# Two early steps of the down projection beside the last channel tile, and that tile's convolution moved behind the third step's operands

## The chip, the core and the metric

The kernel runs on one core of a Trainium2 chip. It uses TensorE (PE, matrix products into PSUM), VectorE (DVE), ScalarE (ACT), GpSimd (POOL) and the sync engine's queue (SP), which issues most of the DMAs. Each engine takes its own instructions strictly in the order in which they stand in its queue and waits at an instruction until what it needs is there. The metric is device microseconds of one execution, the median of several runs, lower is better.

## What is computed

One encoder layer over 256 prompt tokens and 1024 sample tokens of width 1024: a mixer, then a convolutional gated feed-forward network, each with its norms and gated residual. The change lies in the second half:

```python
def conv_ffn(h, w_up, w_conv, b_conv, w_down):
    up = h @ w_up                                   # 1024 -> 2 * 2816 channels
    up = depthwise_conv_of_width_3(up, w_conv) + b_conv
    gate, val = jnp.split(up, 2, axis=-1)
    return (jax.nn.silu(gate) * val) @ w_down       # 2816 -> 1024
```

## The kernel before

**Products in two halves.** Every float32 operand is split in two fp32r parts, a rounded "hi" part (written by ACT, line 90) and the remainder "lo" (written by POOL or DVE, line 91). A product is three matmuls: hi by hi, hi by lo, lo by hi. An operand is complete when both parts are written, and the second or third matmul waits for the lo part.

**The up stage** (lines 1161 to 1257) walks over 22 channel tiles of 128 channels, f. For the sample tokens, which are held in two halves of 512, the two by two block product of weights and tokens is done with seven products of 12 matmuls each instead of eight (a Strassen form with weight sums S1 to S4, tiles `S`). The order on PE is X, Y, X, V, X, V, X: the PSUM banks X and V are accumulated further after they have been copied out, so the next product into a bank waits for the copy. ACT copies X to `ug` (lines 1221 and 1227), V to `uv` (1229) and X again (1237), DVE adds Y to `ug` (1223), X to `uv` (1231), V to `ug` (1233). Then comes the convolution: ACT makes `ag` and `av` with the middle tap (line 1050), DVE adds two taps to each (line 1046, four instructions of 128x1023), ACT applies Silu to `ag` (1247), DVE multiplies (1249), and the product goes to DRAM as `g_d[f]` (line 1079). Tiles 10 to 21 come first, with the prompt tokens merged in, then tiles 0 to 9; tile 9 is the last.

**The down stage** (lines 1259 on) is again a Strassen form, over token halves by column halves: seven products M3, M5, M1, M7, M4, M2, M6, each of which sums over 11 steps k (channel tiles 2k and 2k+1) with 5 token tiles of three matmuls, 15 matmuls for a step. For each step `ops_of` loads the `A` tile of `g_d` (lines 1297 and 1306) and the `w_down` tiles (`raw_d`, `B`, line 1323), forms sums on DVE (`saM`, `sbM`, line 1354) and splits them into `aoM` (128x640) and `boM` (128x512). The `raw` tiles have four slots; a load waits until its slot's last reader is done. M3's step needs one `A` tile and the difference of two weight tiles.

**The early step.** Of M3 the step k=0 (`NE = 1`) is prepared during the up stage: `early_load` (1128) loads `ea` and the two weight tiles `raw_e` when tile 9 begins to be issued, `early_split` (1137) forms the difference and splits both (`eao`, `ebo`). PE runs its 15 matmuls right behind tile 9's last product, ahead of tile 9's convolution. The other steps follow after the up stage's pools are closed.

**Order.** PE, ACT, DVE and POOL follow a scheduler which places an instruction by its estimate of when it can run, within limits; `tc.issue_after(x)` keeps what is issued under it behind instruction x in its engine's queue. So the early split need not stand beside tile 9 because the code says so there. At the very end the residual rows `xo` are loaded by SP (line 1396, three buffers for five row tiles) and added by DVE.

Of the kernel before, what the change touches and what calls it, by code (L numbers as in the profile page):

```python
# [34 lines left out]
def encoder_kernel(ctx: ExitStack, tc: tile.TileContext, x_prompt, x_sample, c_prompt, c_sample,  # L35
# [53 lines left out]
    def split(w, raw, eng=None):  # L89
        nc.scalar.activation(w[:, 0, :], raw, AF.Copy)  # L90
        (eng or nc.gpsimd).tensor_tensor(out=w[:, 1, :], in0=raw, in1=w[:, 0, :].bitcast(F32), op=ALU.subtract)  # L91

# [1044 lines left out]
    def early_split():  # L1137
        for k, (a, b) in enumerate(eops):
            nc.vector.tensor_tensor(out=b[0], in0=b[0], in1=b[1], op=ALU.subtract)
# [4 lines left out]
            eops[k] = [[t[:, h, :] for h in range(2)] for t in (ao, bo_)]  # L1144

# [14 lines left out]
    for f in order:  # L1160
# [10 lines left out]
        def wop(name, src, eng=None):  # L1171
            if wstate["i"] % 8 < 6:
                w = fslot(f"ws{f}_{name}")
            else:
                w = sf.tile([P, 2, 512], F32R, tag="w", name=f"ws{f}_{name}", bufs=2)
            wstate["i"] += 1
            split(w, src, eng)
            wops[name] = w
# [41 lines left out]
        prod(X, "11", "11", True, False)  # L1220
        nc.scalar.activation(ug[:, lo], X, AF.Copy)
        prod(Y, "12", "21", True, True)
        nc.vector.tensor_tensor(out=ug[:, lo], in0=Y, in1=ug[:, lo], op=ALU.add)
        if merged:
# [22 lines left out]
        nc.scalar.activation(ag, ag, AF.Silu)
        conv(av, uv, f + NFF, 1024)
        nc.vector.tensor_tensor(out=av, in0=ag, in1=av, op=ALU.mult)
        store_g(f, av, P, 512)  # L1250
        if merged:
# [5 lines left out]
            store_g(f, accs[1], 0, P)  # L1257
    gst.pop(0)()
    sf_close()
    h2_close()  # L1260
    hb_close()
    er_close()
# [24 lines left out]
    for k in range(NK - 1, NE - 1, -1):  # L1287
        new_ar(0, k)
        if k < 7:
            new_br(k)  # L1290
    loaded, late_b = set(), []

    def load_a(r, c, k):
        if r == c:
# [4 lines left out]
        if r and k >= NPC:
            t = ares[(1, k - NPC)]  # L1300
            if ("a10", k) in loaded:
                return t
            loaded.add(("a10", k))
        else:
            t = new_as(f"A{r}{c}_{k}")
        nc.sync.dma_start(t, g_d[2 * k + c][r])
        return t

    def load_b(c, n, k):
        if c and n and ("b", k) in loaded:  # L1310
# [12 lines left out]
        nc.sync.dma_start(raw, w_down[P * f:P * f + P, 512 * n:512 * n + 512])  # L1323
        return raw
# [169 lines left out]
```

## Time and profile before

| | |
|---|---|
| median of three runs | 1441.95 us (1436.35 to 1443.69) |
| the profiled execution | 1439.31 us |
| its span | 1437.6 us |
| PE busy | 1365.7 us, 95% |
| DVE, ACT, POOL busy | 1022.0, 675.2, 546.9 us |
| up stage, sample-only tiles: one tile | 19.04 us on PE (7 x 12 matmuls) |
| down stage: one step | 15 matmuls, 3.40 us on PE |

The table is read from the left of the engines to the bound: PE is at work in 95% of the span, so what counts are the stretches in which PE waits, and the stretches in which its clock is granted at half speed (the column PEclk of the profile). A busy PE at half clock looks just as busy, so the second kind is found by comparing the starts of equal groups of matmuls.

### The profile page before, as it was taken

How to read it: one execution, taken by the hardware profiler on the slowest of the kernel's cores; microseconds unless marked ns; L12 is line 12 of the kernel's file. 1: busy time of each engine (PE TensorE's matmuls, PEld its weight loads, DVE VectorE, ACT ScalarE, POOL GpSimd, SP SyncE). 2: the span in 40 equal slices, each digit the busy share in tenths (PEclk: the TensorE clock that was granted, in tenths of full speed). 3: DMA queues.
4: the chain of work that ended last, by engine and by line, in shares of the span. 5: the costliest groups of instructions: out<-in, count | busy, mean ns of one | idle time of the engine just before them, and what ended most of it. 6: DMA issues, size and time to landing. Idle time of an engine off the chain costs nothing. (4 is left out here: it accounts for less than half of the span.)

```text
span 1437.6 us, 20261 instructions
## 1 busy us (share of the span) xinstructions
PE 1365.7 (95%) x7057; PEld 1127.9 (78%) x7057; DVE 1022.0 (71%) x1604; ACT 675.2 (47%) x1374; POOL 546.9 (38%) x664
## 2 busy tenths in 40 slices
PE   8999888898999999888999999999999989999996
PEld 5787666676788788887888888887888778888885
DVE  5677668878745556896756566677788676898686
ACT  4544466554333334565445454455444444434642
POOL 3346655787754111434333333333444200000311
PEclk9999999999999999999999999999999999999998
DMA  9648542332233632552221212122222369365443
GB/s 338 215 172 285 197 138 77 104 110 71 81 114 113 212 111 81 169 151 85 66 79 58 85 56 80 61 67 92 89 88 81 111 230 330 114 206 182 92 125 132
DMA packets 174410, 188.63 MB, mean 131 GB/s; under 512 B 11752, under 2 KB 131620, under 8 KB 172004
## 3 DMA queue, kind: packets, MB, share of 16 engines
q1 hardware_dynamic: 166440, 168.24, 36.5%
q10 hardware_dynamic: 6188, 15.69, 3.1%
q0 software_dynamic: 1680, 3.41, 1.3%
q8 instruction: 55, 0.90, 0.3%
q14 instruction: 47, 0.39, 0.1%
HBM read 149.27 MB, written 38.03 MB: 130 GB/s over the span
## 5 line engine op out<-in xcount | busy, mean ns | idle before, releaser
L1156 PE MATMUL dn<-boM,aoM 128*128 128x512 f32 x1140 | 261.5, 391 | 4.7 <-ACT boM L90 4.5
L1156 PEld LDWEIGHTS dn<-boM,aoM 128*128 128x128 f32 x1140 | 215.1, 189 | 51.1 <-ACT boM L90 5.0
L91 POOL TENSOR_TENSOR ws<-raw_s,ws 128x512 fp32r<-128x512 f32 x56 | 89.1, 1594 | 166.6 <-ACT ws L90 165.4
L91 POOL TENSOR_TENSOR ws_S<-S,ws_S 128x512 fp32r<-128x512 f32 x66 | 101.1, 1536 | 128.2 <-ACT ws_S L90 128.2
L1214 PE MATMUL upX<-bop_T,ws_S 128*128 128x512 f32 x528 | 130.8, 397 | 6.8 <-ACT ws_S L90 3.3
L1214 PEld LDWEIGHTS upX<-bop_T,ws_S 128*128 128x128 f32 x528 | 100.4, 192 | 28.5 <-ACT ws_S L90 3.5
L337 PE MATMUL ps_gb<-w_b,h1hi 128*128 128x512 f32 x320 | 104.8, 408 | 1.6 <-DVE w_b L91 1.1
L337 PE MATMUL ps_ga<-w_a,h1hi 128*128 128x512 f32 x320 | 103.6, 402 | 2.0 <-POOL w_a L91 1.0
L90 ACT ACTIVATE ws_S<-S 128x512 fp32r<-128x512 f32 x88 | 54.8, 629 | 77.3 <-PE upX L1214 27.6
L1046 DVE SCALAR_TENSOR_TENSOR ag<-ug,c,ag 128x1023 f32<-128x1023 f32 x44 | 67.7, 1539 | 24.1 <-ACT ag L1050 23.4
L337 PEld LDWEIGHTS ps_ga<-w_a,h1hi 128*128 128x128 f32 x320 | 58.8, 189 | 19.9 <-issue 4.2
L90 ACT ACTIVATE ws<-raw_s 128x512 fp32r<-128x512 f32 x78 | 48.5, 626 | 54.3 <-issue 29.9
L1205 PEld LDWEIGHTS upQ<-hp,ws 128*128 128x128 f32 x576 | 72.3, 191 | 1.9
L1100 PE MATMUL upP<-hp,wp 128*128 128x256 f32 x480 | 63.2, 293 | 10.3 <-DVE wp L91 8.5
L1205 PE MATMUL upQ<-hp,ws 128*128 128x256 f32 x576 | 72.8, 283 | 0.0
L90 ACT ACTIVATE aoM<-saM 128x640 fp32r<-128x640 f32 x50 | 36.8, 738 | 74.1 <-PE dn L1156 34.4
L1100 PEld LDWEIGHTS upP<-hp,wp 128*128 128x128 f32 x480 | 61.0, 200 | 12.2 <-DVE wp L91 9.6
L1182 DVE TENSOR_TENSOR S<-raw_s,raw_s 128x512 f32<-128x512 f32 x44 | 52.3, 1189 | 24.0 <-DMA raw_s<-in_w_up_dram 20.1
L337 PEld LDWEIGHTS ps_gb<-w_b,h1hi 128*128 128x128 f32 x320 | 57.8, 191 | 14.5 <-issue 2.6
L97 POOL TENSOR_TENSOR rstd<-ms,mhalf 128x2 f32<-128x2 f32 (+1 forms) x90 | 65.9, 732 | 7.3
L1214 PE MATMUL upV<-bop,ws_S 128*128 128x512 f32 x264 | 65.1, 397 | 1.8 <-ACT uv L1229 1.8
L883 PE MATMUL y<-wo,mh 128*128 128x512 f32 x160 | 64.0, 400 | 1.8 <-ACT mh L797 1.8
(291 smaller groups left out, 3210.7 us busy)
## 6 DMA issues: line engine op xcount, KB each, us to landing
raw_s<-in_w_up_dram SPq DMA_DIRECT2D x88, 256.0 KB, 3.0
raw_d<-in_w_down_dram SPq DMA_DIRECT2D x82, 256.0 KB, 3.9
A<-g_d SPq DMA_DIRECT2D x55, 320.0 KB, 4.8
wa<-in_w_ada_dram SPq DMA_DIRECT2D x16, 1024.0 KB, 5.1
g_d<-av SPq DMA_DIRECT2D x21, 512.0 KB, 3.0
raw_p<-in_w_up_dram SPq DMA_DIRECT2D x40, 256.0 KB, 3.9
wa<-in_w_ada_dram SPq DMA_DIRECT2D x16, 512.0 KB, 5.4
vr_d<-vr SPq DMA_DIRECT2D x20, 256.0 KB, 2.3
```

The source lines that it names most:

```text
L90: nc.scalar.activation(w[:, 0, :], raw, AF.Copy)
L91: (eng or nc.gpsimd).tensor_tensor(out=w[:, 1, :], in0=raw, in1=w[:, 0, :].bitcast(F32), op=ALU.subtract)
L97: nc.gpsimd.tensor_tensor(out=r, in0=ms, in1=mhalf.to_broadcast([P, n]) if n > 1 else mhalf, op=ALU.pow)
L337: nc.tensor.matmul(ps, st, mv, start=(i == 0), stop=(i == n - 1))
L883: nc.tensor.matmul(ys[n], mh[:, kt, :], wos[(kt, n)][:, 0, :], start=(i == 0), stop=False)
L1046: nc.vector.scalar_tensor_tensor(out=acc[:, o:o + b - a], in0=src[:, a:b], scalar=c2[:, i, fi:fi + 1], in1=acc[:, o:o + b - a], op0=ALU.mu ...
L1100: nc.tensor.matmul(ps[:, half, :], st, hp[:, hi, kt, :], start=(kt == 0 and i == 0 and half == 0), stop=(kt == KT - 1 and i == 2), skip_gr ...
L1156: nc.tensor.matmul(ps, ao[ai][:, cs_], w[wi], start=(first and k == 0 and q == 0), stop=(k == NK - 1 and q == 2), skip_group_check=True)
L1182: nc.vector.tensor_tensor(out=s, in0=a, in1=b, op=op)
L1205: nc.tensor.matmul(Q[:, half, :], st, hp[:, hi, kt, :], start=(kt == 0 and i == 0 and half == 0), stop=(kt == KT - 1 and i == 2), skip_gro ...
L1214: nc.tensor.matmul(ps, w[:, wi, P * j:P * j + P], bops[(b, j)][:, hi, :], start=(start and j == 0 and i == 0), stop=(stop and j == 3 and i ...
```

## The change

`NE` becomes 2: steps k=0 and k=1 of M3 are prepared early, with k=1's `ea` in the same single buffer as k=0's. The `ebo` tiles now take slots of the ring of up weights (`ws_slot`). The early split is held behind two instructions of tile 9: ACT's first copy of X and DVE's first add of Y. Tile 9's convolution, Silu, product and store become a function `glu`, which for tile 9 is called only after the operands of step k=2 have been issued, and is held behind their last instructions. The pools that the convolution uses are closed later, so the load of the gate rows (`G2`) is issued later as well. Last, the loads of `xo` are held behind the last load of the down stage.

```diff
     def split(w, raw, eng=None):
-        nc.scalar.activation(w[:, 0, :], raw, AF.Copy)
-        (eng or nc.gpsimd).tensor_tensor(...)
+        wstate["hi"] = nc.scalar.activation(w[:, 0, :], raw, AF.Copy)
+        wstate["lo"] = (eng or nc.gpsimd).tensor_tensor(...)
...
-    NE = 1
+    NE = 2
...
             nc.vector.tensor_tensor(out=b[0], in0=b[0], in1=b[1], op=ALU.subtract)
-            ao = er.tile([P, 2, 640], F32R, name=f"eao_{k}")
-            bo_ = er.tile([P, 2, 512], F32R, name=f"ebo_{k}")
-            split(ao, a, nc.vector)
+            if k < 2:
+                t = er.tile([P, 2, 640], F32R, name=f"eao_{k}")
+                ao = [t[:, h, :] for h in range(2)]
...
+            bo_ = ws_slot(f"ebo_{k}")
+            nc.scalar.activation(ao[0], a, AF.Copy)
+            nc.vector.tensor_tensor(out=ao[1], in0=a, in1=ao[0].bitcast(F32), op=ALU.subtract)
             split(bo_, b[0], nc.vector)
...
         prod(X, "11", "11", True, False)
-        nc.scalar.activation(ug[:, lo], X, AF.Copy)
+        x_at = nc.scalar.activation(ug[:, lo], X, AF.Copy)
         prod(Y, "12", "21", True, True)
-        nc.vector.tensor_tensor(out=ug[:, lo], in0=Y, in1=ug[:, lo], op=ALU.add)
+        y_at = nc.vector.tensor_tensor(out=ug[:, lo], in0=Y, in1=ug[:, lo], op=ALU.add)
...
         if last_f:
-            early_split()
+            with tc.issue_after(x_at.ins), tc.issue_after(y_at.ins):
+                early_split()
...
-        conv(ag, ug, f, 1024)
...
+        def glu(f=f, ug=ug, uv=uv):
...
+            conv(ag, ug, f, 1024)
...
+        if not last_f:
+            glu()
...
+    dn_ops = {NE: ops_of(0, NE)}
+    with tc.issue_after(wstate["hi"].ins), tc.issue_after(wstate["lo"].ins):
+        glu()
+    gst.pop(0)()
...
-        nc.sync.dma_start(xo, out_rows(t))
+        with tc.issue_after(last_ld[0].ins):
+            nc.sync.dma_start(xo, out_rows(t))
```

What this does to the queues is seen at three places. First ACT's queue. Before, the hi part of `ebo_0` stands in tile 8's work, between two copies out of PSUM that PE waits for (`ug8`, `uv8`; `ws9` are tile 9's weights, `raw_e0_0` the early weight tile); the split of `ea_0` stands still further ahead, in tile 1's work.

```order
L1227 ACTIVATE ug8_10655<-upX_8_10652 128x512
L90 ACTIVATE ws9_S1_10789<-S1_9_10782 128x512
L90 ACTIVATE ebo_0_10903<-raw_e0_0_10771 128x512
L1229 ACTIVATE uv8_10656<-upV_8_10654 128x512
L90 ACTIVATE ws9_S3_10794<-S3_9_10792 128x512
```

Now, in the same queue, both early steps stand in tile 9, k=1's two parts right ahead of the copy of V, and tile 9's `ag` and `av` come behind step 2's operands.

```order
L1228 ACTIVATE ug9_10814<-upX_9_10811 128x512
L1147 ACTIVATE eao_0_10908<-ea_0_10769 128x640
L90 ACTIVATE ebo_0_10909<-raw_e0_0_10771 128x512
L1234 ACTIVATE ug9_10814<-upX_9_10811 128x512
L90 ACTIVATE ebo_1_10916<-raw_e1_0_10777 128x512
L1147 ACTIVATE eao_1_10915<-ea_1_10775 128x640
L1236 ACTIVATE uv9_10815<-upV_9_10813 128x512
L1244 ACTIVATE uv9_10815<-upX_9_10811 128x512
L90 ACTIVATE aoM3_2_11003<-A00_2_10995 128x640
L90 ACTIVATE aoM3_3_11059<-A00_3_10993 128x640
L90 ACTIVATE boM3_2_11006<-sbM3_2_11001 128x512
L1050 ACTIVATE ag9_11009<-ug9_10814,c2_5064 128x1024
```

So the early instructions (two on ACT, three on DVE) have left tiles 1 and 8, and the convolution stands behind step 2. Second DVE's queue at the end of tile 9; before, the five instructions of the convolution stand ahead of every operand of the down stage.

```order
L1233 TENSOR_TENSOR ug9_10808<-upV_9_10807,ug9_10808 128x512
L1046 SCALAR_TENSOR_TENSOR ag9_10928<-ug9_10808,c2_5064,ag9_10928 128x1023 x2
L1046 SCALAR_TENSOR_TENSOR av9_10929<-uv9_10809,c2_5064,av9_10929 128x1023 x2
L1249 TENSOR_TENSOR av9_10929<-ag9_10928,av9_10929 128x1024
L91 TENSOR_TENSOR aoM3_1_11004<-A00_1_10986,aoM3_1_11004 128x640
L1354 TENSOR_TENSOR sbM3_1_11002<-raw_d01_1_10999,B11_1_10987 128x512
L91 TENSOR_TENSOR aoM3_2_11031<-A00_2_10984,aoM3_2_11031 128x640
L91 TENSOR_TENSOR boM3_1_11007<-sbM3_1_11002,boM3_1_11007 128x512
```

Now, in the same queue, step 2's operands are ahead of the taps, and step 3's `boM` behind them.

```order
L1240 TENSOR_TENSOR ug9_10814<-upV_9_10813,ug9_10814 128x512
L91 TENSOR_TENSOR aoM3_2_11003<-A00_2_10995,aoM3_2_11003 128x640
L1356 TENSOR_TENSOR sbM3_2_11001<-raw_d01_2_10998,B11_2_10996 128x512
L91 TENSOR_TENSOR aoM3_3_11059<-A00_3_10993,aoM3_3_11059 128x640
L91 TENSOR_TENSOR boM3_2_11006<-sbM3_2_11001,boM3_2_11006 128x512
L1356 TENSOR_TENSOR sbM3_3_11057<-raw_d01_3_11054,B11_3_10994 128x512
L1046 SCALAR_TENSOR_TENSOR ag9_11009<-ug9_10814,c2_5064,ag9_11009 128x1023
L1046 SCALAR_TENSOR_TENSOR av9_11010<-uv9_10815,c2_5064,av9_11010 128x1023
L1046 SCALAR_TENSOR_TENSOR ag9_11009<-ug9_10814,c2_5064,ag9_11009 128x1023
L1046 SCALAR_TENSOR_TENSOR av9_11010<-uv9_10815,c2_5064,av9_11010 128x1023
L91 TENSOR_TENSOR boM3_3_11062<-sbM3_3_11057,boM3_3_11062 128x512
L1258 TENSOR_TENSOR av9_11010<-ag9_11009,av9_11010 128x1024
```

The convolution has thus passed five operand instructions and now stands ahead of the rest of step 3 and of step 4. Third SP's queue, from tile 7's store on; before, four weight tiles, tile 8's store and then M3's `A` and `B` tiles follow.

```order
L1079 DMA g_d7_71<-av7_10605 128x2x512
L1323 DMA raw_d01_1_10999<-in_w_down_dram 128x512
L1323 DMA raw_d01_2_11026<-in_w_down_dram 128x512
L1323 DMA raw_d01_3_11053<-in_w_down_dram 128x512
L1323 DMA raw_d01_4_11080<-in_w_down_dram 128x512
L1079 DMA g_d8_72<-av8_10749 128x2x512
L1297 DMA A00_1_10986<-g_d2_66 128x640
```

Now, in the same queue, the second early step's loads come in: its `ea_1` stands behind a weight tile that waits for the slot of `raw_e0_0`.

```order
L1079 DMA g_d7_71<-av7_10605 128x2x512
L1134 DMA raw_e1_0_10777<-in_w_down_dram 128x512
L1134 DMA raw_e1_1_10778<-in_w_down_dram 128x512
L1079 DMA g_d8_72<-av8_10749 128x2x512
L1328 DMA raw_d01_2_10998<-in_w_down_dram 128x512
L1131 DMA ea_1_10775<-g_d2_66 128x640
L1328 DMA raw_d01_3_11054<-in_w_down_dram 128x512
L1328 DMA raw_d01_4_11081<-in_w_down_dram 128x512
L1328 DMA raw_d01_5_11108<-in_w_down_dram 128x512
L1302 DMA A00_2_10995<-g_d4_68 128x640
```

The `A` and `B` tiles have moved behind `ea_1` and four weight tiles. PE's queue differs in one thing only: 15 of M3's matmuls read `ebo` and `eao` in place of `boM` and `aoM`. From M5's first operands on, DVE, ACT and POOL have the same order as before, and SP has only the first three `xo` loads further back, behind the last weight tile.

More of the change, by code (lines that the diff above doesn't have):

```diff
@@ L89, in split @@
     def split(w, raw, eng=None):
-        nc.scalar.activation(w[:, 0, :], raw, AF.Copy)
-        (eng or nc.gpsimd).tensor_tensor(out=w[:, 1, :], in0=raw, in1=w[:, 0, :].bitcast(F32), op=ALU.subtract)
+        wstate["hi"] = nc.scalar.activation(w[:, 0, :], raw, AF.Copy)
+        wstate["lo"] = (eng or nc.gpsimd).tensor_tensor(out=w[:, 1, :], in0=raw, in1=w[:, 0, :].bitcast(F32), op=ALU.subtract)
     def rstd_of(pl, ssq, n, scale, eps, tag):
@@ L1139, in early_split, with ws_slot @@
             nc.vector.tensor_tensor(out=b[0], in0=b[0], in1=b[1], op=ALU.subtract)
-            ao = er.tile([P, 2, 640], F32R, name=f"eao_{k}")
-            bo_ = er.tile([P, 2, 512], F32R, name=f"ebo_{k}")
-            split(ao, a, nc.vector)
-            split(bo_, b[0], nc.vector)
-            eops[k] = [[t[:, h, :] for h in range(2)] for t in (ao, bo_)]
+            if k < 2:
+                t = er.tile([P, 2, 640], F32R, name=f"eao_{k}")
+                ao = [t[:, h, :] for h in range(2)]
+            else:
+                ao = [wp.tile([P, 2, 512], F32R, tag="w", name=f"eao{'hl'[h]}_{k}", bufs=5)
+                      .rearrange("p a c -> p (a c)")[:, 0:640] for h in range(2)]
+            bo_ = ws_slot(f"ebo_{k}")
+            nc.scalar.activation(ao[0], a, AF.Copy)
+            nc.vector.tensor_tensor(out=ao[1], in0=a, in1=ao[0].bitcast(F32), op=ALU.subtract)
+            split(bo_, b[0], nc.vector)
+            eops[k] = [ao, [bo_[:, h, :] for h in range(2)]]
+    def ws_slot(name):
+        i = wstate["i"] % 8
+        wstate["i"] += 1
+        return fslot(name) if i < 6 else sf.tile([P, 2, 512], F32R, tag="w", name=name, bufs=2)
     banks = {"i": 0}
@@ L1171, in wop @@
         def wop(name, src, eng=None):
[L1172 to L1176, printed above, removed]
+            w = ws_slot(f"ws{f}_{name}")
             split(w, src, eng)
@@ L1243, in encoder_kernel @@
                     mmk(pss0[j], *eops[k], j, k)
-        ag = sf.tile([P, 1024], F32, tag="ag", name=f"ag{f}", bufs=1)
-        av = sf.tile([P, 1024], F32, tag="av", name=f"av{f}", bufs=2)
-        conv(ag, ug, f, 1024)
[L1247 to L1250, printed above, removed]
+        def glu(f=f, ug=ug, uv=uv):
+            ag = sf.tile([P, 1024], F32, tag="ag", name=f"ag{f}", bufs=1)
+            av = sf.tile([P, 1024], F32, tag="av", name=f"av{f}", bufs=2)
+            conv(ag, ug, f, 1024)
+            nc.scalar.activation(ag, ag, AF.Silu)
+            conv(av, uv, f + NFF, 1024)
+            nc.vector.tensor_tensor(out=av, in0=ag, in1=av, op=ALU.mult)
+            store_g(f, av, P, 512)
+        if not last_f:
+            glu()
         if merged:
@@ L1257, in encoder_kernel @@
             store_g(f, accs[1], 0, P)
[L1258 to L1261, printed above, removed]
     er_close()
@@ L1267, in encoder_kernel @@
     dr, dr_close = pool("dr", side="right")
-    dn, dn_close = pool("dn")
     half_tiles = ((0, 2, 3, 4, 5), (1, 6, 7, 8, 9))
-    Gbc2 = dn.tile([P, 2, D], F32, name="G2")
-    nc.scalar.dma_start(Gbc2.rearrange("p s c -> p (s c)"), gate_d[1].to_broadcast([P, 2 * D]))
     ares, bres = {}, {}
@@ L1290, in encoder_kernel @@
             new_br(k)
-    loaded, late_b = set(), []
+    loaded, late_b, last_ld = set(), [], [None]
     def load_a(r, c, k):
@@ L1305, in load_a @@
             t = new_as(f"A{r}{c}_{k}")
-        nc.sync.dma_start(t, g_d[2 * k + c][r])
+        last_ld[0] = nc.sync.dma_start(t, g_d[2 * k + c][r])
         return t
@@ L1322, in load_b @@
             raw = raw_tile(f"raw_d{c}{n}_{k}")
-        nc.sync.dma_start(raw, w_down[P * f:P * f + P, 512 * n:512 * n + 512])
+        last_ld[0] = nc.sync.dma_start(raw, w_down[P * f:P * f + P, 512 * n:512 * n + 512])
         return raw
@@ L1333, in encoder_kernel @@
     negated, chained = ("M5", "M2"), ("M1", "M7", "M6")
-    y, ygs = {}, {}
-    last_yg = [None]
-    ssq = {t: dn.tile([P, 2], F32, name=f"fssq{t}") for t in range(NT)}
     done = set()
@@ L1368, in ops_of @@
         return [[t[:, h, :] for h in range(2)] for t in (ao, wo_)]
+    dn_ops = {NE: ops_of(0, NE)}
+    with tc.issue_after(wstate["hi"].ins), tc.issue_after(wstate["lo"].ins):
+        glu()
+    gst.pop(0)()
+    sf_close()
+    h2_close()
+    hb_close()
+    dn, dn_close = pool("dn")
+    Gbc2 = dn.tile([P, 2, D], F32, name="G2")
+    nc.scalar.dma_start(Gbc2.rearrange("p s c -> p (s c)"), gate_d[1].to_broadcast([P, 2 * D]))
+    y, ygs = {}, {}
+    last_yg = [None]
+    ssq = {t: dn.tile([P, 2], F32, name=f"fssq{t}") for t in range(NT)}
     def finish(t, n):
@@ L1438, in encoder_kernel @@
         for k in range(0 if i else NE, NK - tail):
-            ops[k] = ops_of(i, k)
+            ops[k] = ops_of(i, k) if i or k > NE else dn_ops[k]
             if i and k == 0:
```

## The prediction

> **What bounds the kernel now.** PE is the bound, and the page and then PE's waits say where it loses time. The list of PE's waits has many short ones in the first half of the program; three belong to the change. Its columns are the total, the number and the longest in us.
>
> ```profile
> span 1437.6 us, 20261 instructions
> ...
> PE dn L1156 <- ACT boM L90: 4.5, 1, 4.5
> ...
> PE upX L1214 <- ACT ug L1221: 2.5, 1, 2.5
> ...
> PE upV L1214 <- ACT uv L1229: 1.8, 1, 1.8
> ```
>
> What a wait costs in all is read from PE's timeline: start, duration, matmuls.
>
> ```profile
> 999.10 2.88 PE L1214 MATMUL upY<-bop,ws 128*128 128x512 f32 x12
> 1004.53 4.61 PE L1214 MATMUL upX<-bop_T,ws_S 128*128 128x512 f32 x12 [2.55 <-ACT ug L1221]
> ...
> 1011.72 2.88 PE L1214 MATMUL upX<-bop_T,ws_S 128*128 128x512 f32 x12
> ...
> 1125.96 2.88 PE L1214 MATMUL upX<-bop_T,ws_S 128*128 128x512 f32 x12
> 1130.61 4.61 PE L1214 MATMUL upV<-bop,ws_S 128*128 128x512 f32 x12 [1.77 <-ACT uv L1229]
> ...
> 1137.80 2.88 PE L1214 MATMUL upX<-bop,ws 128*128 128x512 f32 x12
> 1140.52 2.88 PE L1214 MATMUL upY<-bop,ws 128*128 128x512 f32 x12
> ...
> 1156.84 3.56 PE L1156 MATMUL dn<-ebo,eao 128*128 128x512 f32 x15
> 1164.94 35.35 PE L1156 MATMUL dn<-boM,aoM 128*128 128x512 f32 x145 [4.54 <-ACT boM L90]
> ```
>
> Undisturbed, 12 matmuls take 2.72 us (1137.80 to 1140.52), so 15 take 3.40. From 999.10 three groups should take 8.16 and end at 1007.26; the next starts at 1011.72: **4.46 us lost**. From 1125.96 three groups should end at 1134.12; the next starts at 1137.80: **3.68 lost**. The early step should end at 1160.24; step 1 starts at 1164.94: **4.70 lost**. Behind that wait the chain has one unbroken run:
>
> ```profile
> 1164.94 179.30 PE dn L1156 x780
> ```
>
> 780 matmuls at 2.72/12 us take 176.80, so another **2.50** is lost in it. That is the granted clock. The stretches show it, with the clock as the number ahead of the DMA share:
>
> ```profile
> 1005.00:1010.00 5.00, 5.00 (x17) 3.93 (x16) 5.00 (x4) 1.46 (x3) 3.59 (x2) 0.66 0.00 0
> 1132.00:1135.00 3.00, 3.00 (x8) 2.30 (x7) 0.40 (x1) 0.00 (x0) 0.95 (x1) 0.50 0.28 98
> 1165.00:1167.00 2.00, 2.00 (x4) 1.38 (x5) 1.91 (x4) 0.75 (x2) 0.00 (x0) 0.50 1.00 307
> ```
>
> Behind each of the three waits PE runs at half clock for a few us; so the lost 4.46 and 3.68 are 2.55 and 1.77 of waiting and 1.91 of slow clock each. [...]
>
> **What the three waits hang on.** ACT's timeline at the first two, and the issue of the early `A` tile:
>
> ```profile
> L1131 SPq DMA_DIRECT2D ea<-g_d x1: 339/339/339, 992.9 to 992.9; - x1
> ...
> 995.80 0.74 ACT L90 ACTIVATE eao<-ea 128x640 fp32r<-128x640 f32 x1 [4.04 <-DMA ea<-g_d]
> ...
> 1129.44 0.63 ACT L90 ACTIVATE ebo<-raw_e 128x512 fp32r<-128x512 f32 x1 [4.89 <-DVE raw_e L1139]
> ```
>
> Both are the early split, put by the scheduler into tiles 1 and 8 before its data had come: ACT stands 4.04 and 4.89 us, and the PSUM copies behind it are late for PE. The third wait is tile 9's convolution on DVE, with the down operands queued behind it:
>
> ```profile
> 1143.77 0.68 DVE L1223 TENSOR_TENSOR ug<-upY,ug 128x512 f32<-128x512 f32 x1
> 1151.67 0.69 DVE L1231 TENSOR_TENSOR uv<-upX,uv 128x512 f32<-128x512 f32 x1 [7.22 <-PE upX L1214]
> ...
> 1156.39 2.60 DVE L1046 SCALAR_TENSOR_TENSOR ag<-ug,c,ag 128x1023 f32<-128x1023 f32 x2 [1.37 <-ACT ag L1050]
> ...
> 1161.67 1.23 DVE L1249 TENSOR_TENSOR av<-ag,av 128x1024 f32<-128x1024 f32 x1
> 1162.81 0.82 DVE L91 TENSOR_TENSOR aoM<-A,aoM 128x640 fp32r<-128x640 f32 x1
> 1163.54 0.69 DVE L1354 TENSOR_TENSOR sbM<-raw_d,B 128x512 f32<-128x512 f32 x1
> 1164.14 0.82 DVE L91 TENSOR_TENSOR aoM<-A,aoM 128x640 fp32r<-128x640 f32 x1
> 1164.92 0.69 DVE L91 TENSOR_TENSOR boM<-sbM,boM 128x512 fp32r<-128x512 f32 x1
> ```
>
> The 7.22 us in front of 1151.67 are free on DVE, and ACT is as free there.
>
> **Part by part.** I keep the clock times of before for tile 9, whose own work is undisturbed.
>
> *The early split leaves tiles 1 and 8.* All its instructions go there, and the list of waits counts these two waits once each, so the other sample-only tiles have none like them. **-4.46 and -3.68.**
>
> *Two steps in tile 9.* Six early DVE instructions, four of ACT, start behind DVE's 1143.77. With 0.60 us from start to start for 512 columns (1163.54 to 1164.14) and 0.73 for 640 (1162.81 to 1163.54): difference 1144.37, `eao_0` lo 1144.97, `ebo_0` lo 1145.71 to 1146.40. SP's weight tile for step 2 waits for that slot, so it leaves at 1146.4 and `ea_1` behind it at about 1146.85. Then DVE has k=1's difference and `ebo_1`, and with ACT stands before `eao_1` until `ea_1` lands. Queued behind it on ACT is the copy of V, on which PE's sixth group waits, due at 1137.80 + 5 x 2.72 = 1151.40. How late is the landing? The first `ea` needed 2.9 us (992.9 to 995.80). The other bound are the median and longest times of the `A` tiles of this stage, in a burst:
>
> ```profile
> DMA to landing us min/median/max: 6.2/6.5/7.1
> ```
>
> In place of that burst `ea_1` has two weight tiles beside it, so I take 3.4, near the first: 1150.25. Then 0.74 for `eao_1` and 0.60 for V: 1151.6, a wait of **+0.2** (0 at 2.9; 3.9 at 7.1). PE then has k=0 and k=1 to run, 1156.84 + 6.80 = 1163.64.
>
> *Step 2 ahead of the convolution.* ACT's row at tile 9's end gives the slots:
>
> ```profile
> 1157.04 0.60 ACT L1237 ACTIVATE uv<-upX 128x512 f32<-128x512 f32 x1 [0.69 <-PE upX L1214]
> 1157.67 1.25 ACT L1050 ACTIVATE av<-uv,c 128x1024 f32<-128x1024 f32 x1
> ```
>
> `aoM` hi of step 2 starts at 1157.67 instead of `av`, ends at 1158.40; on DVE `aoM` lo 1158.45, `sbM` 1159.18, step 3's `aoM` lo 1159.78, `boM` lo 1160.56 (0.78 behind, as 1164.14 to 1164.92), complete at 1161.25. PE wants it at 1163.64: the third wait is covered with 2.4 us to spare, and its clock loss goes. **-4.70 and -2.50.** If that cover failed, the price were the two again.
>
> *The convolution between step 3's sum and its `boM`.* What is late next is this. `sbM` of step 3 at 1161.17, then four taps of 1.28 (1156.39 to 1158.95 are two, the next pair's start is 2.56 on): 1161.78 + 5.12 = 1166.90, `boM` lo complete at 1167.59. PE has run steps 0 to 2 at 1156.84 + 10.20 = 1167.04 and one matmul, 0.23, with the hi parts: **+0.3** of wait. Step 4: 1167.5 + 1.14 for the product + 0.61 + 0.73 + 0.69 = 1170.7, wanted at 1167.34 + 3.40 + 0.23 = 1170.97. From there DVE needs 0.60 + 0.73 + 0.61 = 1.94 a step against PE's 3.40, and regains its lead. G2, the store of `g_d[9]` and the weights of steps 7 to 10 now share the DMAs here; I put **+0.3** for that, between nothing and the rival below.
>
> *`xo` behind the last load.* Nothing. SP's last weight tiles are out at 1403.3; three loads behind them at the 4.2 to 6.0 us that these rows need land by about 1410, and DVE's first use is at 1419.85. The end is as before, the fourth and fifth `xo` waiting for a buffer:
>
> ```profile
> 1368.00 35.28 SPq L1323 DMA_DIRECT2D raw_d<-in_w_down_dram  x15
> ...
> DMA to landing us min/median/max: 4.2/5.1/6.0
> ...
> 1419.85 1.41 DVE xo L1401 x2
> ...
> 1428.38 4.21 DMA xo<-out_dram
> ```
>
> Where they stood before (behind `A` loads of M5) PE did not wait, so nothing is gained either.
>
> **The sum.** -4.46 - 3.68 - 4.70 - 2.50 = -15.34; +0.2 + 0.3 + 0.3 = +0.8; in all **-14.5 us**. The profiled execution took 1439.31 us, 1.7 around its span, which gives 1424.8. The three runs have a median of 1441.95 and spread over 7.3; with the profiled one the four have a mean of 1440.3, and from there I forecast 1425.8, rounded to **1426**.
>
> **The rivals.**
>
> *The late `ea_1`.* If it lands as slowly as the `A` rows, 6.5 us, V is copied at 1146.85 + 6.5 + 1.34 = 1154.7: PE waits 3.3 and then runs at half clock, 1.91 to 2.5. Against it: the burst is behind it. The gain falls by some 5.5, 1431.
>
> *Steps 3 to 6 wait on the convolution and the loads behind it.* Step 7's second weight tile gets its slot when step 4's sum is made, 1169.3, and the weight tiles of this stage land in:
>
> ```profile
> DMA to landing us min/median/max: 4.3/5.1/6.0
> ```
>
> So at 1173.6 to 1175.3; `boM` of step 6 stands behind step 7's sum, its `aoM` and M5's first sum (0.60 + 0.73 + 0.73) and takes 0.69: 1176.4 to 1178.1, wanted at 1177.8. If step 3, 4 and 6 each wait a good 1 us and each brings the slow clock of 1.91, 9 us come back: 1435.
>
> *Half the up stage's gain stays away,* since DVE or POOL is late in tile 1 or 8 for another reason: 4 us less, 1430. Nothing in the rows speaks for it; against it, each of the two waits stands once in the list.
>
> *The clock does not follow short waits.* Then the two 1.91s have another cause and stay: 3.82 less gain, 1429.6. Against it, the slow stretches stand right behind the waits. [...]
>
> *Slower.* M3 becomes paced by the four weight slots: steps 7 to 10 each wait for a slot that a sum two steps earlier frees, and for a landing. To lose 15.3 and 7.2 more, each of these four steps would have to be 3.7 us late besides 1.91 of clock: 22.5, 1448. That decides from landings of about 10 us on for all four, against 4.3 to 6.0 in the row above.
>
> *The change not doing what it says* is out: the queues show the moves.
>
> **How the numbers follow.** Forecast 0.68, late `ea_1` 0.11, steps 3 to 6 0.09, half the up gain 0.06, the clock 0.03, slower 0.03. About 0.5%, 7.2 us, is what a measurement of this kernel can tell from no change. The first, second, fourth and fifth give more; the third, at 1435, lies on the line and with the scatter of the runs counts mostly as no change: faster 0.87, same 0.10, slower 0.03. The range goes from 1420 (the lowest run less the full 15.3 is 1421) to 1435, where the third case stands.
>
> **What would show it.** In the changed profile: tiles 1 and 8 at 19.04 us with full clock; no half clock at the start of the down stage; PE's wait before the sixth group of tile 9 under 0.5 us and on ACT's copy of V; one on `boM` of step 3, under 1 us; the last 11 us unchanged. A clock of 0.50 anywhere in tile 9 or M3 makes the forecast wrong by some 2 to 6 us; a PE wait that stays in tile 1 or 8 makes it wrong by 4.

## The result and the profile after

The changed kernel takes **1429.79 us** (median of five runs, 1426.73 to 1431.41) against 1441.95 (1436.35 to 1444.13, five runs): ratio 0.9915, 95% interval 0.990 to 0.993. That is faster by more than the 0.5% bound and 3.8 us above the forecast of 1426, inside the range of 1420 to 1435. The profiled execution has a span of 1428.1 us against 1437.6.

Of the three waits that the prediction dealt with, none is left in the list of PE's waits. In the stretch of the change there is one new one, on `boM` (total, number and longest in us).

```profile
span 1428.1 us, 20261 instructions
...
PE dn L1167 <- DVE boM L91: 2.2, 1, 2.2
```

PE's timeline (start, duration, matmuls) of the changed kernel: the first product of tiles 2, 3, 8 and 9, then the down stage.

```profile
997.82 2.88 PE L1221 MATMUL upX<-bop,ws 128*128 128x512 f32 x12
1016.86 2.88 PE L1221 MATMUL upX<-bop,ws 128*128 128x512 f32 x12
...
1112.06 2.88 PE L1221 MATMUL upX<-bop,ws 128*128 128x512 f32 x12
1131.10 2.88 PE L1221 MATMUL upX<-bop,ws 128*128 128x512 f32 x12
1150.14 6.96 PE L1167 MATMUL dn<-ebo,eao 128*128 128x512 f32 x30
1156.94 14.01 PE L1167 MATMUL dn<-boM,aoM 128*128 128x512 f32 x61
1173.12 42.25 PE L1167 MATMUL dn<-boM,aoM 128*128 128x512 f32 x178 [2.16 <-DVE boM L91]
```

Tiles 2 and 8, among whose products PE stood before, take 19.04 us each, as all others do. (The prediction names the first of them by the early split that stood in the way, which lay in tile 1's work on ACT.) Steps 0 and 1 (30 matmuls, 6.80 us) are followed without a gap by step 2 at 1156.94. But 61 matmuls of 2.72/12 us later, at 1170.77, PE stops in step 6 until 1173.12. The rows of DVE that lead up to it begin with the taps of the moved convolution:

```profile
1154.94 1.28 DVE L1046 SCALAR_TENSOR_TENSOR ag<-ug,c,ag 128x1023 f32<-128x1023 f32 x1
1156.13 1.28 DVE L1046 SCALAR_TENSOR_TENSOR av<-uv,c,av 128x1023 f32<-128x1023 f32 x1
...
1159.72 0.68 DVE L91 TENSOR_TENSOR boM<-sbM,boM 128x512 fp32r<-128x512 f32 x1
...
1167.33 0.82 DVE L91 TENSOR_TENSOR aoM<-A,aoM 128x640 fp32r<-128x640 f32 x1
1171.63 0.83 DVE L1356 TENSOR_TENSOR saM<-A,A 128x640 f32<-128x640 f32 x1 [3.48 <-DMA A<-g_d]
1172.38 1.29 DVE L91 TENSOR_TENSOR boM<-sbM,boM 128x512 fp32r<-128x512 f32 x2
```

DVE was done with step 7's `aoM` at 1168.15, and of steps 6 and 7 only the two `boM` were left to write. Ahead of them in its queue stands `saM`, the first sum of the *next* product M5, and that waits 3.48 us for an `A` tile. In the trace of before, that sum comes behind the last `boM` of M3:

```profile
1187.71 0.69 DVE L91 TENSOR_TENSOR boM<-sbM,boM 128x512 fp32r<-128x512 f32 x1
1188.32 0.82 DVE L1354 TENSOR_TENSOR saM<-A,A 128x640 f32<-128x640 f32 x1
```

The section on the change has DVE's order from M5's first operands on as the same as before. That does not hold: this sum has moved ahead of the `boM` of M3's steps 6 to 10. The chain of waits has the tile's flight and the run of PE behind it:

```profile
1163.07 8.47 DMA A<-g_d
1173.12 161.49 PE dn L1167 x704
```

704 matmuls at 2.72/12 us take 159.57, so 1.92 are lost besides. The stretches around the wait follow (the length, then for PE, its weight loads, DVE, ACT and POOL the busy time with the number of instructions; the last three numbers are the granted clock, the DMA share and GB/s):

```profile
1170.27:1173.68 3.41, 1.25 (x6) 0.71 (x5) 2.03 (x3) 0.74 (x1) 0.00 (x0) 1.00 1.02 365
1173.68:1177.09 3.41, 3.41 (x9) 2.66 (x8) 2.79 (x5) 1.20 (x2) 0.00 (x0) 0.50 0.95 319
1177.09:1180.50 3.41, 3.41 (x16) 2.82 (x15) 3.39 (x6) 1.50 (x4) 0.00 (x0) 1.00 0.99 342
```

The account of the two traces: up stage -8.14; down stage from PE's first to its last matmul 269.80 us before (1156.84 to 1426.64), 266.95 now (1150.14 to 1417.09), -2.85; what lies behind it 10.96 and 11.01; and the part ahead of tile 1, which the change does not touch, +1.44 (978.78 against 977.34). The sum is -9.5. That last term is scatter: in the other profiled executions of this study tile 1 starts anywhere from 975.39 to 980.75.

### The profile page after: what moved, and what is told of

It is laid out like the page before. It is cut to its first block, busy times and chain, and to the rows that moved or that the text cites. A ratio compares the mean times of both kernels' runs of the same rounds, so it can differ in the third digit from the quotient of the medians.

```text
span 1428.1 us, 20261 instructions
## 1 busy us (share of the span) xinstructions
PE 1363.6 (95%) x7057; PEld 1126.8 (79%) x7057; DVE 1021.8 (72%) x1604; ACT 675.0 (47%) x1374; POOL 546.7 (38%) x664
## 3 DMA queue, kind: packets, MB, share of 16 engines
q0 software_dynamic: 1680, 3.41, 1.4%
## 4 chain that ended last, share of the span: by engine, by line
PE 66%; DVE 12%; DMA 6%; POOL 6%; issue 5%; ACT 4%; SPq 0%; POOLq 0%; ACTq 0%; DVEq 0%
PE upX L1221 17%; PE dn L1167 14%; PE upV L1221 8%; PE upQ L1212 5%; PE upY L1221 4%; PE ps_gb L337 3%; PE ps_qkS L346 3%; PE y L883 2%; PE y L884 2%; PE y L886 2%; PE ps_ga L337 2%; DVE St L727 1%; POOL rstd L97 1%; DMA raw_p<-in_w_up_dram 1%; PE ps_qkP L346 1%
## 5 line engine op out<-in xcount | busy, mean ns | idle before, releaser
L1167 PE MATMUL dn<-boM,aoM 128*128 128x512 f32 x1125 | 257.7, 391 | 2.4 <-DVE boM L91 2.2
L1167 PEld LDWEIGHTS dn<-boM,aoM 128*128 128x128 f32 x1125 | 212.0, 189 | 48.0 <-DVE boM L91 2.6
L1100 PE MATMUL upP<-hp,wp 128*128 128x256 f32 x480 | 62.1, 290 | 12.2 <-DVE wp L91 9.2
L337 PE MATMUL ps_gb<-w_b,h1lo 128*128 128x512 f32 x160 | 64.8, 405 | 0.0
```

The source lines that it names most:

```text
L337: nc.tensor.matmul(ps, st, mv, start=(i == 0), stop=(i == n - 1))
L1100: nc.tensor.matmul(ps[:, half, :], st, hp[:, hi, kt, :], start=(kt == 0 and i == 0 and half == 0), stop=(kt == KT - 1 and i == 2), skip_gr ...
L1167: nc.tensor.matmul(ps, ao[ai][:, cs_], w[wi], start=(first and k == 0 and q == 0), stop=(k == NK - 1 and q == 2), skip_group_check=True)
```

## The experiments

Theory: the change gains by the pins, which hold the early split in tile 9 (tiles 2 and 8), and by the second early step (start of the down stage), and gives some 4 us back at step 6, because `boM` stands behind M5's first sum. Rivals: the moved convolution itself is what makes step 6 late; the load of G2 does it by delaying the `A` tile; the wait is an accident of one execution.

**1. The pins alone, one early step.** Before, with the early split pinned:

```diff
-        nc.scalar.activation(ug[:, lo], X, AF.Copy)
+        x_at = nc.scalar.activation(ug[:, lo], X, AF.Copy)
...
-            early_split()
+            with tc.issue_after(x_at.ins), tc.issue_after(y_at.ins):
+                early_split()
```

> The kernel before with one edit: the early split of its single early step is held behind tile 9's first copy of X and first add of Y. Theory: the waits in tiles 1 and 8 with their slow clock are 4.46 and 3.68 us and both belong to the early split's place alone, so this gives 8.1 us (about 1434 against 1442), with the 4.5 us wait at the start of the down stage and its half clock still there. Rival: DVE or POOL is late in those tiles for another reason, then one of the waits stays and it gives about 4 us.

1432.86 us (1430.11 to 1433.79) against 1439.02 (1435.52 to 1441.12) of before on the same chip: ratio 0.9955, interval 0.994 to 0.997. PE's timeline:

```profile
978.16 2.88 PE L1214 MATMUL upX<-bop,ws 128*128 128x512 f32 x12
...
1149.52 3.56 PE L1156 MATMUL dn<-ebo,eao 128*128 128x512 f32 x15
1157.62 2.80 PE L1156 MATMUL dn<-boM,aoM 128*128 128x512 f32 x5 [4.54 <-ACT boM L90]
```

From 978.16 to 1149.52 are nine tiles of 19.04: both stalls of the up stage are gone with the pins alone, and the wait at the start of the down stage stays. In the trace that is the -8.14 expected. In the medians it is -6.2, with an interval of 4.3 to 8.6 us less than before, so 8.14 is not excluded; experiments 8 and 10 show a possible reason for a difference.

**2. The convolution where it was.** The changed kernel, with tile 9's convolution issued right behind its tile:

```diff
-        if not last_f:
-            glu()
+        glu()
...
-    with tc.issue_after(wstate["hi"].ins), tc.issue_after(wstate["lo"].ins):
-        glu()
```

> The changed kernel with tile 9's convolution called at its old place, so ahead of all operands of the down stage; two early steps, pins and xo as changed. Theory: the second early step covers 3.4 of the 4.7 us that the convolution cost, step 2 waits about 1.5 us and the half clock behind it costs 1.9; DVE then takes step 6's boM ahead of M5's first sum, so the 4.3 us lost at step 6 of the changed kernel are gone. In all the same time as the changed kernel within 1 us. Rival: moving the convolution is what removes the third wait, then this is 4 to 7 us slower than the changed kernel.

1428.04 us (1423.98 to 1428.22), ratio 0.9917 (0.9902 to 0.9932): the changed kernel's ratio of 0.9915, as the theory had it, but not quite for its reasons. PE's timeline:

```profile
1150.74 6.96 PE L1167 MATMUL dn<-ebo,eao 128*128 128x512 f32 x30
1158.11 0.49 PE L1167 MATMUL dn<-boM,aoM 128*128 128x512 f32 x1 [0.41 <-ACT boM L90]
1159.39 55.83 PE L1167 MATMUL dn<-boM,aoM 128*128 128x512 f32 x245 [0.78 <-DVE boM L91]
```

Two things work against each other. With the convolution first, step 2 is late: the gaps are 0.57 (1157.54 to 1158.11) and 1.05 (1158.34 to 1159.39), and no half clock follows. But the wait at step 6 is gone, since with the convolution elsewhere the scheduler puts M5's first sum behind all of M3's steps. From the first down matmul to the last one's end it takes 264.57 us, 2.4 less than in the changed kernel's trace. So the second early step alone covers most of the third wait, and moving the convolution, as it is done in this change, brought nothing that the medians show.

**3. M5's first sums behind M3's last operand.**

```diff
+            if i == 1 and k == 0:
+                m3_lo = wstate["lo"].ins
-            ops[k] = ops_of(i, k) if i or k > NE else dn_ops[k]
+            with tc.issue_after(m3_lo) if i == 1 and k < 2 else ExitStack():
+                ops[k] = ops_of(i, k) if i or k > NE else dn_ops[k]
```

> The changed kernel with M5's operands of steps 0 and 1 held on DVE behind M3's last operand; nothing else on DVE or ACT moves. Theory of the order: PE's 2.16 us wait at step 6 is there because step 6's boM stands on DVE behind M5's first sum, which nobody needs for another 20 us; with the sum further back the wait and its slow clock go and the time falls by 4.2 us against the changed kernel, although the A tiles of that sum still land over 7 us after their issue. Rival of the bandwidth: the DMAs are full from 1163 to 1175, so the weight tiles of steps 7 to 9 come late too, PE waits there instead, and 0 to 1 us is won.

1425.52 us (1424.82 to 1427.23), ratio 0.991 (0.9896 to 0.9924). DVE's timeline at the same place:

```profile
1168.23 1.28 DVE L91 TENSOR_TENSOR boM<-sbM,boM 128x512 fp32r<-128x512 f32 x2
1173.46 0.69 DVE L1356 TENSOR_TENSOR sbM<-raw_d,raw_d 128x512 f32<-128x512 f32 x1 [3.94 <-DMA raw_d<-in_w_down_dram]
```

Both `boM` are written at once, and DVE now waits where nobody waits for it. PE runs the down stage without a gap until the last copies: 262.81 us, 4.1 less than the changed kernel. G2, the store of `g_d[9]` and the weights are issued as before, so it takes the order on DVE to make PE wait; neither the convolution nor the transfers do it by themselves.

**4. G2 later.** The load of G2 (1 MB) moved behind step 4 of M5:

```diff
-    nc.scalar.dma_start(Gbc2..., gate_d[1].to_broadcast([P, 2 * D]))
...
+            if i == 1 and k == 4:
+                with tc.issue_after(wstate["hi"].ins):
+                    nc.scalar.dma_start(Gbc2..., gate_d[1].to_broadcast([P, 2 * D]))
```

> The changed kernel with the 1 MB load of the gate rows G2 issued in M5 instead of in M3 (its place on ACT is behind M5's step 4); the scheduler also puts step 6's boM ahead of M5's first sum in this one, so the wait at step 6 should be gone by either theory, 4.2 us less than the changed kernel. What it tells is the landing of M5's first A tiles: theory of G2, without its 1 MB beside them they land in 4 to 6 us in place of 8.5; rival, the store of g_d[9] and the weight tiles fill the DMAs as well and they still need 7 or more.

1424.80 us (1422.24 to 1427.41), ratio 0.9902 (0.9885 to 0.9919); 262.91 us for the down stage, no wait. The scheduler, without G2 there, also put M5's first sum behind `boM` of steps 6 to 8, so nothing waited for the tile, and no view gives its landing. But the traces keep every DMA packet with its size. The two `A` tiles of that sum are 256 packets of 2560 bytes, and they are the next of that size to move after their issue. In the changed kernel they run from 1165.84 to 1170.85, and G2's packets of 8192 bytes run beside them from 1167.11 to 1171.42; the last one ends 7.8 us after the issue of the second tile (1163.07). In experiment 3, with G2 at the same place, it is 7.3 us. Here they run from 1167.88 to 1170.01, and the last one ends 5.0 us after the issue (1165.03). So in these three executions G2 is what draws the landing out, by 2.3 to 2.8 us. Without that, step 6's `boM` would have been complete at about 1170.7 in the changed kernel, an estimate (1173.0 less 2.3), and PE wants it at 1170.77. The wait at step 6 thus takes both: the sum ahead of `boM`, and G2 beside the tile.

**5. The `xo` loads not held back.**

```diff
-        with tc.issue_after(last_ld[0].ins):
-            nc.sync.dma_start(xo, out_rows(t))
+        nc.sync.dma_start(xo, out_rows(t))
```

> The changed kernel with the xo loads no longer held behind the last weight load, so that they stand among M5's and M1's A tiles on SP as before. Theory (the pin brings nothing): PE's waits, the step-6 wait of about 2.2 us among them, and the last 11 us (10.96 in before, 11.01 in the changed kernel) stay as they are; time within 1 us of the changed kernel. Rival (the pin is worth something, since three 512 KB loads no longer push M5's A tiles back): a PE wait appears in M5 or M1, and the time is 2 us or more above the changed kernel.

1427.68 us (1426.04 to 1429.74), ratio 0.9919 (0.9904 to 0.9934), beside the changed kernel's 1428.49 in experiment 7 on the same chip. Three loads leave at 1197 to 1205 instead of 1394, no PE wait appears in M5 or M1, the part behind PE is 10.6 us. No gain of the pin shows. One thing was not expected: the wait at step 6 had no slow clock behind it (PE's timeline, then the chain):

```profile
1174.48 40.89 PE L1167 MATMUL dn<-boM,aoM 128*128 128x512 f32 x179 [1.56 <-DVE boM L91]
```

```profile
1174.48 159.91 PE dn L1167 x704
```

159.91 for 704 matmuls is full clock: at 2.72/12 us each they take 159.57, and with the slow stretch of the changed kernel they took 161.49.

**6. Two early steps without the pins.**

```diff
-            with tc.issue_after(x_at.ins), tc.issue_after(y_at.ins):
-                early_split()
+            early_split()
```

> The changed kernel without the two pins on the early split: both steps stay, and the scheduler puts their ACT and DVE instructions where it likes, which is tile 1 (eao of the first step), tile 3 (eao of the second) and tile 8 (both ebo). Theory (the pins make the gain of the up stage): ACT stands about 4 us for each ea and about 5 for raw_e, PE waits in tiles 1, 3 and 8, each wait with 1.9 us of half clock behind it, so tiles 1 and 3 take about 23.5 us and tile 8 about 22.7 in place of 19.04: +12.6 us, time about 1442 where the changed kernel takes 1429.8. Rival (early tiles without pins wait no more once the second step is there, or the waits come from elsewhere): tiles of 19.04 us and the changed kernel's time.

1435.26 us (1433.17 to 1439.78), ratio 0.9978 (0.9966 to 0.999): 6.8 us more than the changed kernel, not 12.6. PE's timeline:

```profile
997.07 2.88 PE L1221 MATMUL upX<-bop,ws 128*128 128x512 f32 x12
1004.50 3.04 PE L1221 MATMUL upX<-bop_T,ws_S 128*128 128x512 f32 x12 [1.84 <-ACT ug L1228]
1018.26 2.88 PE L1221 MATMUL upX<-bop,ws 128*128 128x512 f32 x12
...
1044.51 3.01 PE L1221 MATMUL upX<-bop_T,ws_S 128*128 128x512 f32 x12 [1.61 <-ACT ug L1228]
...
1134.71 3.02 PE L1221 MATMUL upX<-bop_T,ws 128*128 128x512 f32 x12 [2.87 <-DVE uv L1238]
```

The three waits are there, so the pins do make the gain of the up stage. But the tiles lose 2.15, 1.90 and 3.17 us: the wait and 0.3 more each, with none of the 1.9 of slow clock that a wait of 1.77 had brought in before. Even the wait at step 6 (2.11 us here) has none behind it, while that of 2.16 us in the changed kernel has. So the length of a wait does not decide. The starts and lengths of the half-clock stretches do have a pattern: all but the last, which begins behind PE's last matmul, are 3.41 us long or twice that, and within one execution they begin at whole multiples of 3.413 us from each other (in the changed kernel, for one, at 586.59, 668.51 and 1173.68: 24.0 and 148.0 times). On such a grid the longest of these waits is cut in two:

```profile
1130.17:1133.58 3.41, 1.67 (x8) 1.05 (x6) 1.98 (x3) 0.63 (x1) 1.22 (x1) 1.00 0.30 96
1133.58:1136.99 3.41, 2.28 (x10) 1.90 (x11) 2.63 (x5) 1.25 (x1) 0.00 (x0) 1.00 0.25 85
```

Neither stretch has PE idle for more than 1.74 us, and the clock stays at 1.00; the changed kernel's wait, shown above, lies whole in one stretch (1.25 busy, 2.16 idle) and the next is at 0.50. Experiments 8 and 10 test that.

**7 and 9. The changed kernel and the kernel of experiment 3 again, on one chip.** No new edits.

> The changed kernel as it is, beside the next one on the same chip. Theory: tiles 1 to 9 at 19.04 us each, one wait of PE of 2 to 2.5 us at step 6 on boM behind M5's first sum, half clock behind it, 266.9 us from the first down matmul to the last one's end. Rival (the wait at step 6 was an accident of one execution, a late landing): no wait at step 6 this time, about 262.8 us.

> The changed kernel with M5's first two operand steps held behind M3's last sum on DVE, once more, beside the changed kernel on the same chip. Theory: no PE wait in the down stage before the last evacuations, 262.8 us from its first matmul to its last, so 4.1 us less than the changed kernel in the trace and about 3 to 5 less in the median. Rival (the 4 us of the down stage do not reach the end of the program): medians within 1.5 us of each other.

1428.49 us (1427.29 to 1429.46), ratio 0.9924 (0.9909 to 0.9939), and 1426.49 (1422.76 to 1427.96), ratio 0.9907 (0.9891 to 0.9923). The second has no wait of PE in the down stage ahead of the last copies. The first one's, in PE's timeline:

```profile
1172.24 42.99 PE L1167 MATMUL dn<-boM,aoM 128*128 128x512 f32 x181 [2.06 <-DVE boM L91]
```

The wait is no accident. In the traces the two differ by 3.9 us (266.75 and 262.82 for the down stage). The medians differ by 2.0, between what theory and rival expected, and the intervals of the ratios overlap. Against before on the same chip the changed kernel has ratios of 0.9915 and 0.9924 and the kernel of experiment 3 of 0.9910 and 0.9907, which is 0.7 and 2.4 us less. So what M5's sum costs is clear in the traces, and it comes out smaller in the medians. A possible reason: the wait at step 6 stands in all six traces with this order on DVE (1.56 to 2.16 us in the result and in experiments 5 to 8 and 10), but only in the changed kernel's own two does half clock follow (at 1173.68 and 1173.65).

**8. Waits by size.** Redundant copies of V on ACT, in tiles 2 to 6:

```diff
-        nc.scalar.activation(uv[:, hi], V, AF.Copy)
+        for _ in range({2: 5, 3: 6, 4: 7, 5: 8, 6: 9}.get(f, 1)):
+            nc.scalar.activation(uv[:, hi], V, AF.Copy)
```

> The changed kernel, where ACT copies V into uv 5, 6, 7, 8 and 9 times in tiles 2 to 6 instead of once, so that PE waits at the fourth product into V. With some 0.55 us for each further copy, against about 1.9 us of slack (copy done at 1028.59, next group on V at 1030.46 in tile 3), the waits should be about 0.9, 1.4, 2.0, 2.5 and 3.0 us. Theory (the clock falls to half for one stretch of 3.41 us when PE stood idle for more than about half of the stretch before, the stretches lying on a fixed grid of their own): none behind 0.9 and 1.4; behind 2.0, 2.5 and 3.0 only where over about 1.75 us of the wait falls into one stretch; a tile with it loses 1.7 to 1.9 us more than its wait. Rival (every wait from 1.77 us up brings the half clock): behind 2.0, 2.5 and 3.0 alike. [...]

1449.06 us in its only execution (before 1437.97). PE's timeline, the first two waits and the tiles around them:

```profile
998.87 2.88 PE L1221 MATMUL upX<-bop,ws 128*128 128x512 f32 x12
1013.92 3.01 PE L1221 MATMUL upV<-bop,ws_S 128*128 128x512 f32 x12 [1.29 <-ACT uv L1237]
1019.50 2.88 PE L1221 MATMUL upX<-bop,ws 128*128 128x512 f32 x12
1035.18 4.62 PE L1221 MATMUL upV<-bop,ws_S 128*128 128x512 f32 x12 [1.92 <-ACT uv L1237]
1042.39 2.88 PE L1221 MATMUL upX<-bop,ws 128*128 128x512 f32 x12
```

The waits became 1.29, 1.92, 2.55, 3.18 and 3.81 us (0.63 for each further copy, where I had put 0.55). The tile with 1.29 loses 1.59; the other four lose their wait and 1.91 to 1.93. So 1.92 us is enough in this kernel. It does not part the theory from the rival: in all four cases one stretch of the grid had PE idle for 1.92 us or more.

**10. Seven waits alike.** The same with seven copies in each of tiles 2 to 8.

> The changed kernel, where ACT copies V into uv 7 times in each of tiles 2 to 8: seven waits of PE of nearly the same length, about 2 us each, 21 us or more from one to the next, so that they lie differently on a grid of 3.41 us. Theory (grid): some are followed by half clock and some are not, 2 to 5 of 7, and those with over about 1.75 us in one stretch are the ones; with 1.7 to 1.9 us lost behind each of those. Rival (the length of the wait decides): all seven alike.

1457.38 us in its only execution (before 1437.97), with seven waits of 2.55 us each. Six tiles take 23.46 to 23.53 us (19.04 + 2.55 + 1.9), tile 6 takes 21.89. PE's timeline in tiles 5 and 6:

```profile
1085.07 4.51 PE L1221 MATMUL upV<-bop,ws_S 128*128 128x512 f32 x12 [2.55 <-ACT uv L1237]
1092.27 2.88 PE L1221 MATMUL upX<-bop,ws 128*128 128x512 f32 x12
1108.59 3.01 PE L1221 MATMUL upV<-bop,ws_S 128*128 128x512 f32 x12 [2.55 <-ACT uv L1237]
1114.16 2.88 PE L1221 MATMUL upX<-bop,ws 128*128 128x512 f32 x12
```

The stretches of the grid at tiles 6 and 7:

```profile
1103.32:1106.73 3.41, 2.71 (x12) 1.90 (x11) 1.93 (x3) 3.27 (x7) 0.69 (x1) 1.00 1.02 330
1106.73:1110.15 3.42, 1.56 (x7) 1.31 (x8) 0.69 (x1) 1.74 (x4) 1.26 (x1) 1.00 0.13 40
...
1127.21:1130.63 3.42, 0.87 (x5) 0.41 (x4) 0.18 (x1) 3.11 (x6) 1.26 (x1) 1.00 0.50 170
1130.63:1134.04 3.41, 3.41 (x9) 2.67 (x10) 0.51 (x1) 0.00 (x0) 0.00 (x0) 0.50 0.00 0
```

The same wait, cut by the grid into 0.70 and 1.85 us of idle, leaves the clock alone; whole in one stretch it halves it. The rival falls: length does not decide. The 1.85 us lie just above the 1.75 that were expected to be enough, so the bound is about half a stretch and no sharper. The number of slow ones, 6 of 7, is above the 2 to 5 expected; those were reckoned for waits of 2 us, and these are longer.

**11 and 12. The kernel of experiment 3 with four `xo` buffers, and without them beside it.**

```diff
-        xo = dn.tile([P, D], F32, tag="xo", name=f"xo{t}", bufs=3)
+        xo = dn.tile([P, D], F32, tag="xo", name=f"xo{t}", bufs=4)
```

> The kernel with M5's first two steps behind M3's last sum, and four buffers for xo instead of three, so that the fifth load of xo leaves when the first tile's second store has landed (SP 1407.60 in the profile of that kernel) and not the second's (1412.22). Theory (the tail hangs on that load and on nothing else): no wait of DVE on xo before the last tile's adds (3.12 us before), the last adds follow the last tile's norm on POOL, about 2.7 us earlier, so that what lies behind PE's last matmul takes about 8 us instead of 11; 2 to 3 us less in the median than that kernel's 1426. Rival (the last stores are the bound whenever the adds are made): the tail stays at 11 us and so does the time.

> The kernel with M5's first two steps behind M3's last sum, as it is, beside the kernel with four xo buffers on the same chip. Theory: 2 to 3 us above that one; PE without a wait from tile 1 to the last evacuations. Rival: the same time as that one.

Four buffers: 1421.92 us (1419.08 to 1425.87), ratio 0.9896 (0.9878 to 0.9913) against 1437.21 of before. Three buffers: 1424.61 (1421.73 to 1425.01), ratio 0.9902 (0.9886 to 0.9918). The first row is the last tile's add on DVE with four buffers, the second with three:

```profile
1412.66 0.75 DVE L1418 SCALAR_TENSOR_TENSOR xo<-y,rf,xo 128x512 f32<-128x512 f32 x1 [0.44 <-POOL rf L1407]
```

```profile
1418.26 0.75 DVE L1418 SCALAR_TENSOR_TENSOR xo<-y,rf,xo 128x512 f32<-128x512 f32 x1 [3.24 <-DMA xo<-out_dram]
```

The add now waits for the norm on POOL and no longer for the load, and what lies behind PE's last matmul shrinks from 10.66 to 7.96 us. The trace gives -2.7, the medians -2.7. The intervals of the ratios overlap, so the medians alone would not settle it; the moved wait does. This is the lowest median of the study.

## Why the prediction was right, and where it was off

- **The early split leaves tiles 1 and 8 (-8.14).** Right in the trace to the hundredth, and by the pins, as experiments 1 and 6 show. What was taken wrongly is that the 1.91 us of slow clock in each belong to the wait for certain. They belong to the wait and to where the grid cuts it. One profiled execution of before had slow clock behind all its three waits; others need not, as experiment 6 shows for waits of the same kind, so the average gain may be less than 8.14: it is 6.2 by the medians of experiment 1, whose interval reaches to 8.6.
- **The late `ea_1` (+0.2).** It was 0. ACT's timeline in tile 9:

```profile
1142.82 0.74 ACT L1147 ACTIVATE eao<-ea 128x640 fp32r<-128x640 f32 x1 [1.81 <-DMA ea<-g_d]
1143.47 0.58 ACT L1236 ACTIVATE uv<-upV 128x512 f32<-128x512 f32 x1
```

  The load left SP at 1139.11, 1.0 us earlier than reckoned (tile 9 runs 6.70 us earlier than before), and landed in 3.71 us, between the 2.9 of the quiet load and the 6.5 of the burst, near the 3.4 taken. The copy of V was done at 1144.05, due at 1144.70.
- **Step 2 ahead of the convolution (-7.20).** Right: no wait and no slow clock at 1156.94. By experiment 2, all but 1.6 us of it comes with the second early step alone.
- **The convolution ahead of step 3's `boM` (+0.3).** It was 0: `boM` was complete at 1160.40, wanted at 1160.57. The four taps, which alternate between `ag` and `av` here, start 1.19 to 1.20 us apart; the 1.28 taken was that of two taps on the same tile.
- **The loads of steps 7 to 10, G2 and the store (+0.3).** This is the step that failed: 2.35 us of wait and 1.92 of slow clock at step 6, 4.1 net by the traces of experiment 3. The slow clock in M3 that the prediction named as a sign of being wrong is there, at 1173.68. The mechanism stood in the prediction, as a rival: "`boM` of step 6 stands behind step 7's sum, its `aoM` and M5's first sum". But it priced step 7's weight tiles as the late ones (1173.6 to 1175.3); these were there, and what was late was M5's `A` tile, 8.47 us in flight against the 6.2 to 7.1 of its nearest row, with G2's packets beside it (experiment 4). The prediction reckoned with no wait on that tile. The rival's 9 us needed three such waits; there was one.
- **`xo` (0).** Right, by experiment 5; and the wait for a fourth buffer, quoted in the prediction as unchanged, was worth 2.7 us in experiment 11.
- **The clock.** The rival that the clock does not follow short waits was given 0.03. Neither it nor the forecast had it right: in these traces the stretches lie on a grid of 3.413 us, and PE idle for about half of one stretch is enough (slow behind 1.77 us in before and 1.92 in experiment 8; not behind 1.74 and 1.85 in experiments 6 and 10, so the bound lies near 1.8 and is not sharper in these rows).

Taken together: -15.3 of gains, of which 1 to 2 us are there only in some executions, and 1.9 (experiment 5, at full clock) to 4.1 lost at step 6. That is 9.2 to 12.4 us, estimated from these terms, against 12.2 and 10.6 in the medians of the two chips. The forecast had 14.5; that 1429.79 is still within its range is because the range was wide enough for one term of this size to fail. In the two traces the gain is 9.5, and of the 5 us that are missing 4.3 are lost at step 6 and 1.4 are the scatter ahead of tile 1; against them stand the 0.8 that were set aside for waits and not needed where they were expected.

## What to carry to other kernels

When a piece of work is moved out of the way, read the queue behind the new place to its end: what cost here was not the moved convolution itself but a sum for the *next* product, which the scheduler now put ahead of two operands that PE needed, and which hung on a load that was still in flight. An engine here takes its queue in order, so one wait delays everything behind it (DVE's 3.48 us at `saM` kept `boM`, behind it in the queue, from starting before 1172.38, and PE stood for 2.16), and operands that are needed next go ahead of anything that hangs on a DMA. And a gain read from one execution's slow clock is to be counted in part only, since the same wait meets it in one execution and not in the next (the wait at step 6 in two traces of six).

## What the runs showed of the hardware that was not expected

- From tile 1 on the granted clock went to 0.50 for one stretch of 3.41 us (two, 6.83 us, at the third wait of before) where PE stood idle for more than some 1.8 us of the stretch before (1.77 in before and 1.92 in experiment 8 were enough, 1.74 in experiment 6 and 1.85 in experiment 10 were not), on a grid that is fixed within an execution and differs between executions (a slow stretch begins at 666.51, 665.49 and 665.89 in the three traces of the kernel of experiment 3). A wait cost its length and 0.30 us (1.84 cost 2.15 in experiment 6), and with a slow stretch behind it 1.6 more (1.92 cost 3.85 in experiment 8). Waits of 1.77 (before) and 1.92 us (experiment 8) met it, waits of 2.11 and 2.87 (experiment 6) and one of 2.55 (experiment 10) did not.
- DVE's taps of 128x1023 started 1.28 us apart on the same tile (before) and 1.19 to 1.20 when they alternated between two (the changed kernel).
- An `A` tile of 320 KB took 8.47 us to land (7.87 to 8.44 in experiments 5, 6 and 7) beside the 1 MB of G2, with a DMA share of 1.05 from 1165 to 1168, against 3.71 for `ea_1`, of the same size, in tile 9. Without G2 beside it its packets were through 2.3 to 2.8 us sooner (experiment 4).
